# Start of a conformer layer laid out by channel and computed in pairs, and a new place on ACT for three weight splits

## Chip, cores and metric

One core of a Trainium2 chip. The metric is the device time of one execution in microseconds (us), the median of the runs of the kernel. It was 1515.53 us (3 runs, 1515.49 to 1515.91) before the change.

## The reference

Two layers on x of 256 tokens by 1024 channels, all in float32, each sub-layer steered by a vector c (adaLN): a convolution module, a dense feed-forward part, then attention and a mixture of experts. The change lies in the first sub-layer and at the start of the second:

```python
c_act = jax.nn.silu(c)
sh1, sc1, g1, sh2, sc2, g2 = jnp.split(c_act @ ada_w[l] + ada_b[l], 6, axis=-1)
h = x * (1.0 + sc1[:, None, :]) + sh1[:, None, :]
a, g = jnp.split(h @ w_in + b_in, 2, axis=-1)
u = a * jax.nn.sigmoid(g)
u = depthwise_conv(u, w_dw, width=31, causal=True) + b_dw
out = jax.nn.silu(layer_norm(u, g_n, b_n)) @ w_out + b_out
x = layer_norm(ALPHA * x + (1.0 + g1[:, None, :]) * out, ln_g[l, 0], ln_b[l, 0])
h = x * (1.0 + sc2[:, None, :]) + sh2[:, None, :]
f = swiglu(h, ffn_w13[0], ffn_w2[0])
```

(`depthwise_conv` stands for the call of `conv_general_dilated`.)

## The kernel before

Every product of float32 values is made of three matmuls (`mm3`, L203 to L207): high half by high half, low half of the weight by high half, high half of the weight by low half. Weights come as tiles of 1 MB (128 x 2048 numbers) from a packed stream, through six raw buffers; SyncE (SP) issues the transfers in order (L173). `split` (L179) makes the high half on ScalarE (ACT, L189), and the low half by a subtraction on VectorE (DVE) or, for the tiles named in `SPLIT_POOL`, on GpSimd (POOL), at L194. Three pairs of buffers hold the halves. The order of work on each engine is set by the framework's scheduler, steered by `after(...)`, which keeps an instruction from being issued ahead of the given ones. TensorE (PE) takes its instructions strictly in the order given to it.

The stretch that the change touches, up to about 172 us, runs so:

- Start (L117 to L157): c, the taps of the depthwise convolution and six small vectors are loaded as rows, and transposed by PE into columns (`dwT`, `cols`). PE multiplies the adaLN weights with c in `Ada.step` (L226), by 1 MB tile: the scale first, four tiles, then the shift. x (`xtm`, L493) is loaded by token and transposed by PE (`to_dmajor`). `modulate` scales it (`hs`, L343 to L347), in high and low halves.
- Input projection: 8 tiles of 256 columns (`ci`), 48 matmuls each (`cip`). The first two (`FIRST`) are multiplied with the scaled x alone; the shift's share of them is computed apart (`shw`, L524, and L531), and added as a bias `cin` (L535). The others wait for the full h. Then the gate: `sg` (L597) and `U` (L600).
- Depthwise convolution of 31 taps, eight blocks of 128 channels shared out between DVE (`cvv`, L553), ACT with POOL (`pr`, L566, and additions into `dw`, L567) and PE (`cv`, L574, with diagonal matrices `dg` that ACT makes, L481).
- Norm of the convolution's output: transposes and statistics (`cn_tr`, L640), square root (`cn_w`, L354), rows of factors (`cn_rows`, L674), the affine step on dw (L683), z = silu (L688) with its high and low halves (L690, L691).
- Output projection `cout_a` with four weight tiles (`cout`); the norm of the result in `post_ln` (L366 to L388, `xh`), transposes (`x_tr`), the affine steps of the next sub-layer (`h_f`, L343, `h_h`, L345) and then the first feed-forward chunk: `ffn_up`, products with the tiles fa (`fap`) and fb.

Of the kernel before, what the change touches and what calls it, by code (L numbers as in the profile page):

```python
# [19 lines left out]
P = 128  # L20
# [24 lines left out]


# [38 lines left out]
def build(ctx: ExitStack, tc: tile.TileContext, a: dict, dbg: dict | None = None):  # L85
# [26 lines left out]
    def sideps(name):  # L112
# [3 lines left out]
    crows = small.tile([KB, P], F32, tag="crows", name="crows", bufs=1)  # L116
    nc.sync.dma_start(crows[:], a["c"][0].rearrange("(k p) -> k p", p=P))  # L117
    dwrows = tmp.tile([124, 2, P], F32, tag="g32", name="dwrows")
    nc.scalar.dma_start(dwrows[:], a["conv_dw_w"][0].rearrange("j (k p) -> (j k) p", p=P)
                        .rearrange("(u r) p -> r u p", u=2))  # L120
# [8 lines left out]
    ps = mmps("ps_c")  # L129
    nc.tensor.transpose(ps[:, :KB], crows[:], ident[:KB, :KB])  # L130
    cact = cpool.tile([P, KB], F32, name="cact")
    nc.scalar.activation(cact[:], ps[:, :KB], AF.Sigmoid)
    nc.vector.tensor_tensor(cact[:], cact[:], ps[:, :KB], op=ALU.mult)
    crep = cpool.tile([P, KB, 32], F32, name="crep")
    nc.vector.tensor_copy(crep[:], cact[:, :, None].to_broadcast([P, KB, 32]))

    rows = tmp.tile([104, P], F32, tag="h32", name="rows")
    off = 0
    for nm, n in (("conv_in_b", 16), ("conv_dw_b", 8), ("conv_norm_g", 8), ("conv_norm_b", 8), ("ln_g", 32),
                  ("ln_b", 32)):  # L140
# [363 lines left out]
    with after(la):  # L504
        conv_diag(CONV_TENSOR[1][0], 0)
# [810 lines left out]
```

## Time and profile before

| | |
|---|---|
| median of 3 runs | 1515.53 us (1515.49 to 1515.91) |
| the profiled execution's own time | 1517.09 us |
| its span | 1515.3 us |
| PE busy | 1468.2 us, 97% of the span |
| DVE busy | 1262.5 us, 83% |
| ACT busy | 980.9 us, 65% |
| POOL busy | 82.8 us, 5% |
| mean granted clock of PE | 0.989 |
| data read and written | 484.51 MB, mean 320 GB/s |

The profile records one execution. A busy share is an average over the span, and the stretches have different limits: windows give the busy time stretch by stretch, the timeline gives single instructions with what ended the idle time before them (in square brackets), and the tile view gives all instructions on one buffer. PEclk is the granted clock of TensorE, 1.00 for 2.4 GHz and 0.50 for 1.2 GHz. Lengths of matmuls overlap, since they are pipelined.

### The profile page before, as it was taken

How to read it: one execution, taken by the hardware profiler on the slowest of the kernel's cores; microseconds unless marked ns; L12 is line 12 of the kernel's file. 1: busy time of each engine (PE TensorE's matmuls, PEld its weight loads, DVE VectorE, ACT ScalarE, POOL GpSimd, SP SyncE). 2: the span in 40 equal slices, each digit the busy share in tenths (PEclk: the TensorE clock that was granted, in tenths of full speed). 3: DMA queues.
4: the chain of work that ended last, by engine and by line, in shares of the span. 5: the costliest groups of instructions: out<-in, count | busy, mean ns of one | idle time of the engine just before them, and what ended most of it. 6: DMA issues, size and time to landing. Idle time of an engine off the chain costs nothing. (4 is left out here: it accounts for less than half of the span.)

```text
span 1515.3 us, 20370 instructions
## 1 busy us (share of the span) xinstructions
PE 1468.2 (97%) x8018; PEld 1213.2 (80%) x8018; DVE 1262.5 (83%) x1271; ACT 980.9 (65%) x944; POOL 82.8 (5%) x86
## 2 busy tenths in 40 slices
PE   6998999999999999999999999999999999999995
PEld 4886899997967787888888888888888888887884
DVE  2897798757776889899888899988889988888886
ACT  5665444344565776777776677776777777777673
POOL 0692100001001000000000000000000000000000
PEclk9999999999999999999999999999999999999998
DMA  9766699856962788999999999999999999999991
GB/s 356 273 282 226 236 359 336 315 223 269 333 248 85 281 342 331 377 361 354 350 355 348 380 360 353 339 369 356 367 373 359 333 361 363 363 367 345 351 358 52
DMA packets 73380, 484.51 MB, mean 320 GB/s; under 512 B 9044, under 2 KB 11452, under 8 KB 17468
## 3 DMA queue, kind: packets, MB, share of 16 engines
q1 hardware_dynamic: 72848, 482.94, 85.0%
q8 instruction: 65, 1.06, 0.3%
q14 instruction: 39, 0.32, 0.1%
q10 hardware_dynamic: 428, 0.18, 0.0%
HBM read 482.04 MB, written 1.05 MB: 319 GB/s over the span
## 5 line engine op out<-in xcount | busy, mean ns | idle before, releaser
L194 DVE TENSOR_TENSOR eu_l<-eu,eu_h 128x2048 fp32r<-128x2048 f32 (+1 forms) x232 | 507.9, 2213 | 41.4 <-ACT eu_h L189 40.8
L189 ACT ACTIVATE eu_h<-eu 128x2048 fp32r<-128x2048 f32 (+1 forms) x232 | 425.6, 1855 | 89.6 <-PE eup L206 62.5
L207 PE MATMUL eup<-eu_l,g_x 128*128 128x512 f32 x896 | 354.2, 397 | 1.9 <-DVE eu_l L194 1.5
L205 PE MATMUL eup<-eu_h,g_x 128*128 128x512 f32 x896 | 350.6, 391 | 1.8 <-ACT eu_h L189 1.8
L206 PE MATMUL eup<-eu_h,g_x 128*128 128x512 f32 x896 | 349.8, 390 | 0.0
L194 DVE TENSOR_TENSOR e_l<-e,e_h 128x2048 fp32r<-128x2048 f32 (+1 forms) x114 | 251.1, 2212 | 26.0 <-ACT e_h L189 25.7
L189 ACT ACTIVATE e_h<-e 128x2048 fp32r<-128x2048 f32 (+1 forms) x114 | 210.2, 1854 | 21.7 <-PE eup L206 19.6
L207 PEld LDWEIGHTS eup<-eu_l,g_x 128*128 128x128 f32 x896 | 168.2, 188 | 44.1 <-DVE eu_l L194 10.4
L205 PEld LDWEIGHTS eup<-eu_h,g_x 128*128 128x128 f32 x896 | 168.4, 188 | 36.0 <-ACT eu_h L189 2.9
L206 PEld LDWEIGHTS eup<-eu_h,g_x 128*128 128x128 f32 x896 | 168.2, 188 | 35.8
L206 PE MATMUL eo<-e_h,egt 128*128 128x512 f32 x440 | 171.9, 391 | 0.0
L205 PE MATMUL eo<-e_h,egt 128*128 128x512 f32 x440 | 171.5, 391 | 0.0
L207 PE MATMUL eo<-e_l,egt 128*128 128x512 f32 x440 | 156.4, 397 | 0.0
L205 PEld LDWEIGHTS eo<-e_h,egt 128*128 128x128 f32 x440 | 82.6, 188 | 18.3 <-ACT e_h L189 0.4
L206 PEld LDWEIGHTS eo<-e_h,egt 128*128 128x128 f32 x440 | 82.6, 188 | 17.5
L207 PEld LDWEIGHTS eo<-e_l,egt 128*128 128x128 f32 x440 | 79.9, 188 | 15.5 <-issue 0.5
L1059 ACT ACTIVATE egt<-ept 128x512 fp32r<-128x512 f32 x56 | 33.2, 592 | 85.7 <-PE ept L1055 85.7
L1051 ACT ACTIVATE es<-eup 128x512 f32<-128x512 f32 x56 | 33.3, 594 | 42.3 <-PE eup L207 42.0
L1086 POOL TENSOR_TENSOR e_last_l<-e_last,e_last_h 128x1024 fp32r<-128x1024 f32 x1 | 3.0, 2993 | 997.2 <-ACT e_last_h L1084 997.2
L1052 DVE TENSOR_TENSOR eg<-es,eup 128x512 f32<-128x512 f32 x56 | 38.3, 683 | 17.6 <-PE eup L207 17.6
L205 PE MATMUL fap<-h_h,fa_h 128*128 128x256 f32 x176 | 48.9, 280 | 0.9 <-DVE h_h L345 0.9
L206 PE MATMUL fap<-h_h,fa_l 128*128 128x256 f32 x176 | 48.9, 279 | 0.0
(399 smaller groups left out, 2400.5 us busy)
## 6 DMA issues: line engine op xcount, KB each, us to landing
eu<-in_stream_dram SPq DMA_DIRECT2D x216, 1024.0 KB
e<-in_stream_dram SPq DMA_DIRECT2D x106, 1024.0 KB
e_w<-in_stream_dram SPq DMA_DIRECT2D x46, 1024.0 KB
fa<-in_stream_dram SPq DMA_DIRECT2D x11, 1024.0 KB
fb<-in_stream_dram SPq DMA_DIRECT2D x11, 1024.0 KB
f<-in_stream_dram SPq DMA_DIRECT2D x11, 1024.0 KB
ekv_w<-in_stream_dram SPq DMA_DIRECT2D x8, 1024.0 KB
eu<-in_stream_dram SPq DMA_DIRECT2D x16, 512.0 KB
```

Source lines behind the costliest of these rows:

```text
L189: ia = nc.scalar.activation(hi[:, ks], raw[:, ks], AF.Copy)
L194: iv = (sub or nc.vector).tensor_tensor(lo[:, ks, us], raw[:, ks, us], hi[:, ks, us].bitcast(F32), op=ALU.subtract)
L205: nc.tensor.matmul(out, lh, rh, start=start, stop=False)
L206: nc.tensor.matmul(out, ll, rh, start=False, stop=False)
L207: return nc.tensor.matmul(out, lh, rl, start=False, stop=stop)
L1051: nc.scalar.activation(s[:], pa[:], AF.Silu)
L1052: nc.vector.tensor_tensor(g[:], s[:], pb[:], op=ALU.mult)
L1059: ia = nc.scalar.activation(ghf, pt[:], AF.Copy)
L1086: (nc.gpsimd if (n, k0) == (1, 0) else nc.vector).tensor_tensor(lo[:, k0:k1], raw[:, k0:k1], hi[:, k0:k1].bitcast(F32), op=ALU.subtract)
```

## The change

- c, the taps, the small vectors and the scale's bias are laid out by channel ahead of the launch (`by_channel`) and loaded with one transfer (`sm`). x is loaded by channel (`xch`); its copy by token (`xtm`), which the residual needs, is loaded after the gate. The transposes at the start go.
- The scale is computed from four tiles of 256 columns (`scale_sum`: 16 matmuls of 64 x 128 each). After each tile one transpose gives the scale of two blocks of channels (`scale_blocks`), ACT and DVE make their `hs`, and PE multiplies these with the first tile (`first_products`: 12 matmuls).
- Three tiles are multiplied with the scaled x alone (`FIRST`), the third in two halves. The shift's share takes 48 matmuls, not 32.
- POOL splits only one tile, `ci4_0`, in two pieces. Half of the diagonals for the second block on PE are made earlier.
- The splits of the third and fourth output weight tile are issued after the last z (`after(iz)`). The first feed-forward splits are issued after the norm's activation and after the affine steps (`ln_act`, `gate`).

Where a kernel line is quoted below it is the new one. On SP, the start of the program; before:

```order
L117 DMA crows<-in_c_dram 8x128
L173 DMA e_w_143<-in_stream_dram 128x2048
L173 DMA e_w_145<-in_stream_dram 128x2048
L173 DMA e_w_147<-in_stream_dram 128x2048
L493 DMA xtm<-in_x_dram 128x2x1024
L173 DMA e_w_174<-in_stream_dram 128x1024 x2
L260 DMA e_b_209<-in_ada_b_dram 128x1x256
L173 DMA ci_0_260<-in_stream_dram 128x1024 x2
L173 DMA e_w_269<-in_stream_dram 128x2048
```

and with the change (`sc` is a tile of scale weights, `xch` the x by channel, `e_w` a tile of shift or scale weights in the old manner):

```order
L130 DMA sm<-in_small_dram 128x368
L161 DMA sc_97<-in_stream_dram 128x2048
L491 DMA xch<-in_xt_dram 128x2048
L161 DMA ci_0_100<-in_stream_dram 128x2048
L161 DMA sc_102<-in_stream_dram 128x2048
L161 DMA sc_104<-in_stream_dram 128x2048
L161 DMA sc_106<-in_stream_dram 128x2048
L161 DMA ci_0_108<-in_stream_dram 128x2048
L248 DMA e_b_407<-in_ada_b_dram 128x1x256
```

The scale came as four tiles of e_w with x between them; now its first tile, x and the first projection tile come ahead of the other three. On ACT, from the square root of the convolution's norm to z; before:

```order
L354 ACTIVATE cn_w<-cn_mv,eps 128x2
L189 ACTIVATE cout_h<-cout_1329 128x2048
L189 ACTIVATE cout_h<-cout_1327 128x2048
L688 ACT_TABLE_LOAD
L688 ACTIVATE z_1411<-dw,cols 128x256 x2
L690 ACTIVATE z_h<-z_1411 128x512
L688 ACTIVATE z_1418<-dw,cols 128x256 x2
L690 ACTIVATE z_h<-z_1418 128x512
```

and with the change:

```order
L342 ACTIVATE cn_w<-cn_mv,eps 128x2
L765 ACT_TABLE_LOAD
L765 ACTIVATE z_1438<-dw,sm 128x256 x2
L767 ACTIVATE z_h<-z_1438 128x512
L765 ACTIVATE z_1445<-dw,sm 128x256 x2
L767 ACTIVATE z_h<-z_1445 128x512
L765 ACTIVATE z_1452<-dw,sm 128x256 x2
L767 ACTIVATE z_h<-z_1452 128x512
L765 ACTIVATE z_1459<-dw,sm 128x256 x2
L767 ACTIVATE z_h<-z_1459 128x512
L177 ACTIVATE cout_h<-cout_1354 128x2048
L177 ACTIVATE cout_h<-cout_1356 128x2048
```

The two high halves of the output weights and the table load have changed places around z. On ACT, at the norm behind the output projection; before:

```order
L189 ACTIVATE fa_1_h<-fa_1_1710 128x2048
L189 ACTIVATE fb_0_h<-fb_0_1818 128x2048
L354 ACT_TABLE_LOAD
L354 ACTIVATE xh_0_w<-xh_mv_1630,eps 128x1
L354 ACTIVATE xh_1_w<-xh_mv_1648,eps 128x1
L388 ACTIVATE xh_1622<-xh_1622,xh_nm_1638,xh_0_w 128x1024
L343 ACTIVATE h_f_1685<-x_tr_1658,aff_B,aff_A 128x256 x2
L343 ACTIVATE h_f_1690<-x_tr_1659,aff_B,aff_A 128x256 x2
L343 ACTIVATE h_f_1695<-x_tr_1660,aff_B,aff_A 128x256 x2
L343 ACTIVATE h_f_1700<-x_tr_1661,aff_B,aff_A 128x256 x2
L189 ACTIVATE fb_1_h<-fb_1_1824 128x2048
```

and with the change:

```order
L342 ACT_TABLE_LOAD
L342 ACTIVATE xh_0_w<-xh_mv_1657,eps 128x1
L342 ACTIVATE xh_1_w<-xh_mv_1675,eps 128x1
L378 ACTIVATE xh_1649<-xh_1649,xh_nm_1665,xh_0_w 128x1024
L177 ACTIVATE fa_1_h<-fa_1_1737 128x2048
L331 ACTIVATE h_f_1712<-x_tr_1685,aff_B,aff_A 128x256 x2
L331 ACTIVATE h_f_1717<-x_tr_1686,aff_B,aff_A 128x256 x2
L331 ACTIVATE h_f_1722<-x_tr_1687,aff_B,aff_A 128x256 x2
L331 ACTIVATE h_f_1727<-x_tr_1688,aff_B,aff_A 128x256 x2
L177 ACTIVATE fb_0_h<-fb_0_1845 128x2048
L177 ACTIVATE fb_1_h<-fb_1_1851 128x2048
```

fa_1_h moved from ahead of the norm to behind its activation, and fb_0_h from ahead of the norm to behind the affine steps.

```diff
-FIRST = 2
-SPLIT_POOL = ("ci2_0", "ci4_0", )
+FIRST = 3
+SPLIT_POOL = ("ci4_0", )
...
-    conv_diag(CONV_TENSOR[0][0], 0)
-    conv_diag(CONV_TENSOR[0][0], 1)
     e00 = ada_group(0, 0, "e00")
-    e00.step(1, 3)
-    nc.sync.dma_start(xtm[:], a["x"][0].rearrange("(t p) d -> p t d", p=P))
-    e00.step(1)
-    cols = columns()
-    xps = to_dmajor(xtm, "x")
-    c00c = ada_cols(e00.done(1), "c00c")
...
+    load_scale(0)
+    nc.sync.dma_start(xch[:], a["xt"])
+    rawf = [load(win.tile(0, KB, in_cols(0), 256), [KB, 256], "ci0_0")]
+    for g in range(1, 4):
+        load_scale(g)
+    rawf.append(load(win.tile(0, KB, in_cols(1), 256), [KB, 256], "ci1_0"))
+    e00.fetch(0)
...
+    def scale_sum(g):
+        with after(*ipe):
+            for k in range(KB):
+                for m in range(2):
+                    ipe[:] = [nc.tensor.matmul(scps[64 * m:64 * m + 64, g * P:(g + 1) * P], crep64[:, k, :],
+                                               raws[g][:, k, m * P:(m + 1) * P], start=(k == 0), stop=(k == KB - 1))]
...
+    scale_sum(0)
+    la, lv = scale_blocks(0)
+    with after(la, lv):
+        wfirst.append(split(rawf[0], [KB, 256], "ci0_0", parts=2))
+    first_products(0)
+    scale_sum(1)
+    for g in range(1, 4):
+        if g < 3:
+            scale_sum(g + 1)
+        la, lv = scale_blocks(g)
+        first_products(g)
+    with after(la, lv):
+        wfirst.append(split(rawf[1], [KB, 256], "ci1_0", parts=2))
+    with after(*ipe):
+        im = dmajor([psfirst[1]], wfirst[1:2], hs)
+    with after(im):
+        e00.step(0)
...
+    im = half(2, 0)
+    with after(im):
+        c00h = ada_cols(e00e, "c00h")
+    half(2, 1)
...
-        with after(*(behind if t > FIRST else [ishp])):
+        with after(*(behind + iu if t > FIRST else [ishp])):
...
+    xtm = act.tile([P, NT, D], F32, tag="xtm", name="xtm")
+    nc.sync.dma_start(xtm[:], a["x"][0].rearrange("(t p) d -> p t d", p=P))
...
+    conv_diag(CONV_TENSOR[1][0], 0)
     conv_tensor(*CONV_TENSOR[0])
...
     for q in (2, 3):
-        wout.append(split(rout[q], [2, D], f"cout{q}", q == 3, behind=[lz]))
+        with after(iz):
+            wout.append(split(rout[q], [2, D], f"cout{q}", q == 3, behind=[lz]))
...
-        wb = colchunk(w13, FF + c0, width, f"fb{c0}")
+        with after(*gate):
+            wb = colchunk(w13, FF + c0, width, f"fb{c0}")
...
-            with after(last[1]):
-                nxt = ffn_up(c0, 512, lead)
+            with after(last[1], *ln_act):
+                nxt = ffn_up(c0, 512, lead, last)
```

## Rows read from the trace of the kernel before

**Rows 1.** First part of the page: busy time, share of the span, instructions.

```profile
PE 1468.2 (97%) x8018; PEld 1213.2 (80%) x8018; DVE 1262.5 (83%) x1271; ACT 980.9 (65%) x944; POOL 82.8 (5%) x86
```

**Rows 2.** Windows: length, busy us (instructions) of PE, PEld, DVE, ACT, POOL, PEclk, DMA share, GB/s.

```profile
24.00:50.00 26.00, 23.89 (x196) 18.31 (x196) 12.41 (x15) 12.62 (x27) 4.85 (x2) 0.88 0.98 382
50.00:93.00 43.00, 41.47 (x393) 37.34 (x392) 37.49 (x72) 30.20 (x56) 34.51 (x34) 1.00 0.52 200
93.00:124.00 31.00, 31.00 (x148) 27.18 (x149) 29.21 (x75) 20.47 (x48) 26.59 (x28) 1.00 0.62 256
124.00:137.00 13.00, 8.64 (x116) 4.63 (x114) 8.22 (x26) 7.05 (x8) 0.00 (x0) 0.96 0.95 339
172.00:1515.00 1343.00, 1318.16 (x6897) 1094.13 (x6897) 1145.34 (x1031) 880.25 (x746) 10.69 (x7) 0.99 0.87 326
```

**Rows 3.** Timeline of PE, 0 to 32 us: start, length, instruction, idle before.

```profile
7.87 1.94 PE L232 MATMUL e_ps<-e_w,crep 128*32 128x256 f32 x16 [2.03 <-DMA e_w<-in_stream_dram]
...
13.03 1.94 PE L232 MATMUL e_ps<-e_w,crep 128*32 128x256 f32 x16 [0.50 <-DMA e_w<-in_stream_dram]
...
30.58 1.07 PE L232 MATMUL e_ps<-e_w,crep 128*32 128x256 f32 x16
```

**Rows 4.** Tiles cip, cv, cvv, dw: ns min/median/max, first and last start, shape.

```profile
L207 PE MATMUL cip<-hs_l,ci_h x32: 278/283/582, 24.6 to 45.4; 128*128 128x256 f32 x32
...
L206 PE MATMUL cip<-h_h,ci_l x96: 276/276/385, 49.9 to 87.2; 128*128 128x256 f32 x96
...
L574 PE MATMUL cv<-U,dg x140: 377/378/483, 92.8 to 123.0; 128*128 128x256 f32 x140
...
L553 DVE SCALAR_TENSOR_TENSOR cvv<-U,dwT,cvv x111: 471/475/491, 58.7 to 120.6; 128x256 f32<-128x256 f32 x111
...
L567 POOL TENSOR_TENSOR dw<-dw,pr x55: 724/736/2847, 61.1 to 110.6; 128x256 f32<-128x256 f32 x55
```

**Rows 5.** Timeline, 126 to 138 us.

```profile
126.90 0.30 ACT L354 ACTIVATE cn_w<-cn_mv,eps 128x2 f32<-128x2 f32 x1 [5.20 <-DVE cn_mv L659]
...
130.82 3.33 DVE L683 TENSOR_TENSOR dw<-dw,cn_rows 128x512 f32<-128x512 f32 x5 [1.45 <-PE cn_rows L674]
...
132.03 1.91 ACT L189 ACTIVATE cout_h<-cout 128x2048 fp32r<-128x2048 f32 x1 [1.93 <-DMA cout<-in_stream_dram]
...
133.96 1.28 ACT L688 ACT_TABLE_LOAD   x1
...
135.25 1.09 ACT L688 ACTIVATE z<-dw,cols 128x256 f32<-128x256 f32 x2
...
137.12 1.22 PE L205 MATMUL cout_a<-cout_h,z_h 128*128 128x512 f32 x2 [3.84 <-ACT z_h L690]
```

**Rows 6.** Windows of the tile cout_a alone.

```profile
137.00:142.60 5.60, 5.48 (x13) 4.32 (x14) 0.00 (x0) 0.50 1.01 420
...
142.60:163.00 20.40, 19.67 (x85) 15.46 (x83) 2.20 (x4) 1.00 0.46 165
```

**Rows 7.** Timeline, 161 to 172 us.

```profile
161.26 1.92 ACT L189 ACTIVATE fb_h<-fb 128x2048 fp32r<-128x2048 f32 x1 [7.64 <-PE cout_a L206]
...
163.19 1.28 ACT L354 ACT_TABLE_LOAD   x1
...
166.95 1.23 ACT L388 ACTIVATE xh<-xh,xh_nm,xh_w 128x1024 f32<-128x1024 f32 x1
...
169.57 1.93 ACT L343 ACTIVATE h_f<-x_tr,aff_B,aff_A 128x256 f32<-128x256 f32 x4 [1.40 <-PE x_tr L330]
...
171.11 0.38 PE L205 MATMUL fap<-h_h,fa_h 128*128 128x256 f32 x1 [0.92 <-DVE h_h L345]
```

**Rows 8.** Windows of the tile cip alone, columns as in rows 2.

```profile
54.80:93.00 38.20, 30.51 (x262) 29.84 (x261) 3.48 (x8) 3.28 (x8) 1.00 0.50 192
```

**Rows 9.** Timeline of DVE, 40 to 82 us.

```profile
45.36 4.27 DVE L345 CAST h_h<-h_f 128x512 fp32r<-128x512 f32 x1 [2.46 <-ACT h_f L343]
...
79.25 2.69 DVE L194 TENSOR_TENSOR ci_l<-ci,ci_h 128x2048 fp32r<-128x2048 f32 x1 [4.30 <-POOL dw L567]
```

More of the change, by code (lines that the diff above doesn't have):

```diff
@@ new lines, in build, with load_scale @@
+    scps = sideps("sc_ps")
+    raws = []
+    def load_scale(g):
+        raws.append(load(e00.w.tile(0, KB, D + g * 256, 256), [KB, 256], f"sc{g}"))
+    load_scale(0)
[5 more added lines that the diff above has]
+    e00.fetch(0)
+    rawf += [load(win.tile(0, KB, in_cols(t), 256), [KB, 256], f"ci{t}_0") for t in range(2, FIRST)]
@@ new lines, in build, with low @@
+    A = small.tile([P, KB], F32, tag="affA", name="aff0_A", bufs=4)
+    dgs[CONV_TENSOR[0][0], 0] = act.tile([P, 16, P], F32, tag="cd", name="dg_first", bufs=4)
+    hs_h = act.tile([P, KB, S], F32R, tag="big0", name="hs0_h")
+    hs_l = [tmp.tile([P, KB // 2, S], F32R, tag="gm", name=f"hs0_l{u}") for u in range(2)]
+    hs = (hs_h, hs_l)
+    psfirst = [accps(f"cip{t}") for t in range(FIRST)]
+    wfirst, im = [], None
+    def low(k):
+        return hs_l[k // 4][:, k % 4, :]
+    ipe, scale_row = [], {}
@@ new lines, in scale_blocks @@
+    def scale_blocks(g):
+        pst = mmps(f"sct{g}")
+        with after(*ipe):
+            ipe[:] = [nc.tensor.transpose(pst[:, :P], scale_row.pop(g)[:], ident[:])]
+        two = slice(2 * g, 2 * g + 2)
+        nc.vector.scalar_tensor_tensor(A[:, two], pst[:, :P].rearrange("p (m r) -> p m r", m=2)[:, :, 0], 1.0, scb[:, two],
+                                       op0=ALU.add, op1=ALU.add)
+        for k in (2 * g, 2 * g + 1):
+            la = nc.scalar.activation(hs_h[:, k, :], xch[:, k, :], AF.Copy, scale=A[:, k:k + 1])
+            lv = nc.vector.scalar_tensor_tensor(low(k), xch[:, k, :], A[:, k:k + 1], hs_h[:, k, :].bitcast(F32),
+                                                op0=ALU.mult, op1=ALU.subtract)
+        return la, lv
@@ new lines, in first_products @@
+    def first_products(g):
+        wh, wl = wfirst[0]
+        with after(*ipe):
+            for k in (2 * g, 2 * g + 1):
+                for f in range(2):
+                    fs = slice(f * P, (f + 1) * P)
+                    im = mm3(psfirst[0][:, f * S:(f + 1) * S], (wh[:, k, fs], wl[:, k, fs]), (hs_h[:, k, :], low(k)),
+                             k == f == 0, k == KB - 1 and f == 1)
+        ipe[:] = [im]
+    scale_sum(0)
+    la, lv = scale_blocks(0)
+    with after(la, lv):
+        wfirst.append(split(rawf[0], [KB, 256], "ci0_0", parts=2))
@@ new lines, in build @@
+    first_products(0)
[7 more added lines that the diff above has]
+        wfirst.append(split(rawf[1], [KB, 256], "ci1_0", parts=2))
+    with after(*ipe):
+        im = dmajor([psfirst[1]], wfirst[1:2], hs)
+    with after(im):
+        e00.step(0)
+    with after(last_split[0]):
+        conv_diag(CONV_TENSOR[0][0], 0)
+    for t in range(2, FIRST):
+        with after(la, lv):
+            wfirst.append(split(rawf[t], [KB, 256], f"ci{t}_0", parts=2))
@@ new lines, in build, with half @@
+    with after(*last_split):
+        conv_diag(CONV_TENSOR[0][0], 1)
+    e00e = e00.done(0)
+    def half(t, f):
+        wh, wl = wfirst[t]
+        for k in range(KB):
+            im = mm3(psfirst[t][:, f * S:(f + 1) * S], (wh[:, k, f * P:(f + 1) * P], wl[:, k, f * P:(f + 1) * P]),
+                     (hs_h[:, k, :], low(k)), k == f == 0, k == KB - 1 and f == 1)
+        return im
+    im = half(2, 0)
+    with after(im):
+        c00h = ada_cols(e00e, "c00h")
+    half(2, 1)
+    xps = [xch[:, 2 * q:2 * q + 2, :].rearrange("p k s -> p (k s)") for q in range(KB // 2)]
```

108 lines of the change are left out of this document (47 added, 61 removed).

## The prediction

> **What bounds the kernel now.** I read the page's busy shares first: TensorE (PE) works 97% of the span [rows 1]. A kernel like that gets faster only where PE waits or works slowly, so the windows come next [rows 2]. Behind 172 us PE is busy 1318 of 1343 us at a DMA share of 0.87, and but for splits of the first feed-forward chunk nothing in the change touches that stretch; of the roughly 172 us ahead of it, PE has 8.6 busy of 13 us at 124 to 137 and works at a mean granted clock of 0.88 at 24 to 50. Both edits lie there, and whatever they save ahead of the second feed-forward chunk shifts all behind it, because from there on both programs have the same order on PE and the stretch hangs on PE. Then the timelines. In the start, three scale tiles of 1 MB are each met by PE as they land, at 7.87 to 13.03 us (2.6 us a tile), and each takes 1.94 us, where the same instructions take 1.07 at 30.58, once the clock is up [rows 3]. Products of the input projection with the scale alone run from 24.6 to 45.4 us, the first ones also at the low clock [rows 4]. Further on PE sits idle 3.84 us for z's high half [rows 5], works its first 13 matmuls of the output projection in 5.6 us at a clock of 0.50 (the 1.2 GHz level), and the rest at 1.00 [rows 6].
>
> **Part B, the scalar engine behind the convolution.** Now ACT does: high half of output weight (1.91, ends 133.94), table load (1.28), two z (1.09, to 136.34), z's high half, and PE starts 0.78 later, at 137.12 [rows 5]. The split waits for its transfer until 132.03, and the table load stands behind it. z itself needs dw, of which DVE makes five steps from 130.82 in 3.33 us, 0.67 each, two to a pair of channel blocks, so the first pair is ready at 130.82 + 2 x 0.67 = 132.15 [rows 5]. With both splits behind all z, the table load stands behind the square root of 126.90 [rows 5] and is over by about 128.5, hidden. Then z runs 132.15 to 133.24 and PE starts 0.78 later, at about 134.0: **-3.1 us**. PE then waits 0.8 instead of 3.84 us, and before had its low clock right behind that idle time. I take it that the clock stays at 2.4 GHz: 13 matmuls at 0.42 (5.48 / 13) become 13 at 0.23 (19.67 / 85) [rows 6], 13 x 0.19 = **-2.5 us**. If the clock still falls, this is nil.
>
> What is queued behind the moved work: the two splits follow z's last half. z takes ACT four times about 1.75 us from 132.15, to 139.2, so the splits end at 141.1 and 143.0, and their low halves on DVE (2.3 each) about 145.6. PE comes to the third weight tile behind 48 matmuls, 134.0 + 48 x 0.23 = 145.0; its products with high halves need only ACT. So I set a wait at nothing, with a bound of 0.6 us above (145.6 - 145.0).
>
> The norm behind the projection: before, fb_h was split on ACT from 161.26 to 163.18 and the table load started at 163.19, after the statistics [rows 7]. With the gate there is nothing ahead of it, worth up to 1.0. In return fa_1_h (1.92) is put between the norm's pass and the affine steps; the transposes of PE run in it, and of the 1.4 us that ACT waited for them [rows 7] it uses the whole and passes it by 0.5. Net **-0.5 us**, from -1.0 to +0.5. Then fb's two high halves come after the affine steps, 3.8 us of ACT, while PE has 96 matmuls of fa to do: hidden. B: 3.1 + 2.5 + 0.5 = **-6.1 us**. Bounds: 3.1 - 0.6 - 0.5 = 2.0 (clock falls, all waits come) and 3.1 + 2.5 + 1.0 = 6.6.
>
> **Part A, the start.** Taken away: the transposes of c, x, the small rows and the taps, and ACT's small transfers; the added 1 MB of x for the residual is read at 50 to 93 us, where the DMA share is 0.52 [rows 2], so it costs nothing. Added: 16 matmuls of 64 columns out by 128 in for each of four scale tiles. Before, a scale tile is 8 of 32 columns by 256, four side by side in the array, and now two side by side; the same numbers pass in twice the time, so a tile takes up to twice 1.94 and 1.07 [rows 3]: I put 3.6 at the low clock and 1.9 at the high one, since the last end counts once. I lay it out at 2.6 us a transfer: scale 0 lands at 7.9, x 10.5, tile 0 13.1, scales 1 to 3 15.7, 18.3, 20.9, tile 1 23.5. PE: scale 0 at the low clock to 11.5; transpose, scale, hs on ACT and DVE; first 12 products 14.4 to 17.5; scale 1 to 20.6; from there I put the clock up (PE has then worked nearly without a break), so scale 2 to 22.5, products of pair 2 to 25, scale 3 to 27, pairs 3 and 4 to 32. Tile 1's split runs to 33.2, its 48 matmuls at 0.115 to 38.7 (before 45.4 [rows 4]). Four shift tiles (1.07 each, [rows 3]) end at about 43, tile 2 in halves with the shift's columns between at 48.4, the shift's 48 products at 53.9, tile 3's low half at 55.2.
>
> So at 55.2 five tiles of 48 remain. Before, at 54.8, 261 of the projection's matmuls remained [rows 8], 21 more than 240. Those 21 are 2.4 us (0.115 each, half of the 0.23 for 512 columns); less 0.4, 2.0 us are won. From 54.8 to the last one's end near 87.5 [rows 4] are 32.7 us, and 261 x 0.115 are 30.0: 2.7 went to other work and waits, and of these I count 2.1 as gone, since the shift's small sums and the low halves are made earlier against their need. The convolution on PE, which starts at 92.8 [rows 4], starts **4.1 us** earlier. Its other parts must keep up. DVE is busy 29.2 of 31 us there [rows 2]; its U waits for the shift 1.8 us longer, but the 4.30 us in which its low half of a tile stood for a POOL addition [rows 9] go, since the last tile's low half is due before POOL's additions bind it. Its taps, last begun at 120.6 [rows 4], then begin their last 1.8 to 2.5 us earlier, near 118.5, and end near 119. POOL's additions, last begun at 110.6 [rows 4], now stand behind some 17 diagonals and one high half of ACT (6.5 us by the order, at 0.29 and 1.9 each) and end near 118, just under the transposes at 119.2. I take **-3.7 us**; bounds: +0.5 (DVE and POOL hold the end where it was and the later U shows) and -5 (tile 3 isn't waited for either).
>
> One row speaks against part A. DVE's cast of 128x512 took 4.27 us, 45.36 to 49.63, while POOL did its low half, and a low half of DVE beside POOL additions 2.69 [rows 9]. The change has POOL's low half of tile 4 at about 54 to 59, beside DVE's low half of tile 3. The Trainium skill ("SBUF — State Buffer", section "SBUF: two separate sides") says that the port pair that the two share is locked for a whole instruction, and that whoever comes second waits it out; the 4.27 us cast agrees with that. I have DVE first, since tile 3's high half precedes tile 4's on ACT, so the sum has nothing for it. If POOL is first, one of its two pieces (about 2.3 us, half of the 4.27) goes ahead of tile 3: -3.7 becomes -1.4.
>
> **Sum.** 6.1 + 3.7 = 9.8 us off a profiled span of 1515.3, which gives 1505.5. The profiled execution took 1517.09, 1.6 above the median of 1515.53; the difference lies around the span, so I take the 9.8 off the median: **1505.7 us**.
>
> **Rivals.**
> 1. *The front gives nothing*: PE reaches the convolution earlier, but DVE (29.2 of 31 busy) or POOL ends as before. For it: those shares. Against: the 4.30 us wait that goes. 1515.5 - 6.1 = 1509.4.
> 2. *The clock falls again at the output projection*, or the third weight tile is late: B is 3.1 + 0.5 = 3.6. 1515.5 - 3.6 - 3.7 = 1508.2. For it: the idle stretch isn't quite gone. Against: it is 0.8 and not 3.84.
> 3. *POOL takes the port first* (above): 1505.7 + 2.3 = 1508.0.
> 4. *The other side: the clock stays low in the front.* PE works in short pieces between transfers and pairs there, and before it was at 0.88 in the mean over 24 to 50 with far longer runs [rows 2]. Each us at the low level from 21 on does half a us of work. From the 9.8 forecast, low to 21 + 19.6 = 41 us is the point at which all gain is eaten; low to 50 costs 14.5: 1520.2. Against: behind 30.58 PE's clock was up, with pieces of products between shift tiles [rows 3].
> 5. *The change doesn't do what it says*: the fine pairs wait on ACT and DVE in turn so that tile 0 ends as late as tile 1 does now. That is rival 1 in its time.
>
> **Chances.** Forecast (1503.5 to 1507) 0.50; rivals 1 and 5 0.17; 2 0.10; 3 0.07; parts lost in both A and B, within 3 us of now, 0.09; rival 4 0.07. The best case is 1515.5 - 6.6 - 5 = 1503.9, and mixes of 1 and 2 come to 1515.5 - 3.6 + 0.5 = 1512.4. The range **1502.5 to 1511.5** goes a little past the best case, whose terms are no exact bounds, and leaves out rival 4 and the worst of the mixes. Within 0.2% (3.0 us, about what a measurement of this kernel can tell from no change): 0.09. Faster 0.84, slower 0.07.
>
> **What would show it.** PE's output projection starts about 7 us earlier and its wait for z's high half is under 1 us (before 3.84); its windows show clock 1.00 throughout; the table load lies before z's dw; the cv tile starts near 88.7, cn_tr near 119.5; the first fap starts near 161.3 (171.11 less 9.8); the stretch behind is the same length. Wrong would be: cv starting early and cn_tr not (rival 1); PEclk 0.50 at the output projection (2); a DVE low half above 4 us near 55 (3); PEclk 0.50 between 25 and 45 (4); or a stretch behind 172 us that has grown, which would mean that transfers set the time there.

## The result, and the profile after

The changed kernel took 1508.48 us, the median of 6 runs (1506.44 to 1511.43), beside 1515.96 us for the kernel before on the same chips (1515.49 to 1520.02). The ratio is 0.9946, with a 95% interval from 0.9931 to 0.9960. A second series, further down, gave 0.9938 (0.9924 to 0.9953). The forecast was 1505.7 us, faster; the range went from 1502.5 to 1511.5. The profiled execution has a span of 1509.4 us, 5.9 less than before.

The windows of the changed kernel, columns as in the rows of before:

```profile
24.00:50.00 26.00, 23.85 (x239) 20.49 (x238) 10.14 (x19) 17.95 (x46) 0.30 (x1) 1.00 0.86 339
50.00:93.00 43.00, 43.00 (x400) 37.90 (x399) 38.63 (x78) 33.39 (x70) 32.03 (x34) 1.00 0.74 286
93.00:124.00 31.00, 30.93 (x165) 26.66 (x167) 28.42 (x75) 20.60 (x48) 26.91 (x29) 1.00 0.51 203
124.00:137.00 13.00, 11.59 (x116) 7.25 (x109) 9.92 (x27) 8.31 (x15) 0.00 (x0) 1.00 0.97 364
172.00:1509.00 1337.00, 1313.50 (x6833) 1089.10 (x6831) 1137.86 (x1023) 876.60 (x741) 10.68 (x7) 0.99 0.87 326
```

Compare these with [rows 2]. PEclk is 1.00 from 24 us on, where it was 0.88 at 24 to 50. At 124 to 137 us PE is busy 11.59 us, not 8.64. The last window has the same DMA share of 0.87; it begins at the same time and ends with the span, so its length shows only that the span is shorter. Counted from the first product of fa, 1344.2 us follow before and 1346.2 now.

The timeline at z, which answers to [rows 5]:

```profile
124.72 0.30 ACT L342 ACTIVATE cn_w<-cn_mv,eps 128x2 f32<-128x2 f32 x1 [5.20 <-DVE cn_mv L736]
...
125.03 1.28 ACT L765 ACT_TABLE_LOAD   x1
...
128.63 3.33 DVE L760 TENSOR_TENSOR dw<-dw,cn_rows 128x512 f32<-128x512 f32 x5 [1.45 <-PE cn_rows L751]
...
130.08 1.09 ACT L765 ACTIVATE z<-dw,sm 128x256 f32<-128x256 f32 x2 [3.77 <-DVE dw L760]
...
131.95 0.97 PE L193 MATMUL cout_a<-cout_h,z_h 128*128 128x512 f32 x3 [0.85 <-ACT z_h L767]
```

The table load now starts at 125.03, right behind the square root. z starts as soon as DVE has made the first pair of dw, and PE starts at 131.95 after 0.85 us of waiting, not 3.84. The first 5.6 us of the output projection, which were at 0.50 [rows 6], read:

```profile
131.90:137.50 5.60, 5.55 (x24) 4.43 (x25) 0.00 (x0) 1.00 0.99 360
```

In the 5.6 us in which PE did 13 matmuls, it now does 24, at 1.00. Behind this, PE never waits for a half of an output weight: the tile view of cout_a has waits for z's halves and for PE alone. The timeline behind the projection, answering to [rows 7]:

```profile
158.74 1.23 ACT L378 ACTIVATE xh<-xh,xh_nm,xh_w 128x1024 f32<-128x1024 f32 x1
...
159.87 1.90 ACT L177 ACTIVATE fa_h<-fa 128x2048 fp32r<-128x2048 f32 x1
...
161.67 1.91 ACT L331 ACTIVATE h_f<-x_tr,aff_B,aff_A 128x256 f32<-128x256 f32 x4
...
163.18 0.39 PE L193 MATMUL fap<-h_h,fa_h 128*128 128x256 f32 x1 [1.20 <-DVE h_h L333]
```

The start, where [rows 3] were scale tiles of another form, as PE sees it:

```profile
6.25 3.29 PE L516 MATMUL sc_ps<-sc,crep 128*64 128x128 f32 x32 [6.25 <-DMA sc<-in_stream_dram]
...
12.45 0.58 PE L193 MATMUL cip<-hs_h,ci_h 128*128 128x256 f32 x1 [2.14 <-ACT ci_h L177]
...
16.35 3.35 PE L516 MATMUL sc_ps<-sc,crep 128*64 128x128 f32 x32
...
20.10 1.97 PE L516 MATMUL sc_ps<-sc,crep 128*64 128x128 f32 x32 [0.40 <-DVE sce L519]
...
28.05 0.39 PE L193 MATMUL cip<-hs_h,ci_h 128*128 128x256 f32 x1 [0.79 <-ACT hs_h L530]
```

Tile 0's products begin at 12.45 us (24.0 before), each later pair of blocks waits 0.79 us for ACT, and the clock rises between the second scale tile (3.35 us) and the third (1.97 us): its mean is 0.60 in the window from 16 to 20 us and 1.00 from 20 to 24. Last, the convolution on PE and the transposes behind it (tile view), for [rows 4]:

```profile
L646 PE MATMUL cv<-U,dg_first x32: 377/378/483, 90.7 to 97.5; 128*128 128x256 f32 x32
...
L716 PE MATMUL cn_tr<-ident,dw x16: 271/272/299, 121.0 to 122.9; 128*128 128x128 f32 x16
```

It starts at 90.7 us, where it was 92.8, and the transposes at 121.0, where they were 123.2.

To compare whole programs, I cut the span at seven starts that the tile views give: the first cn_tr, the first and last product of the output projection (cout_a), the first of fa, the first of ff_a (behind the second chunk's products), the last of wo_a and the first of eup (expert products). The table has the length of each stage in us, good to 0.1, from one profiled execution of each kernel; the kernels are described with the experiments.

| kernel | to cn_tr | to cout_a | cout_a | to fa | to ff_a | to end of wo_a | to eup | the rest |
|---|---|---|---|---|---|---|---|---|
| before | 123.2 | 13.9 | 25.3 | 8.7 | 44.7 | 274.5 | 16.7 | 1008.3 |
| changed | 121.0 | 10.9 | 23.0 | 8.3 | 46.1 | 275.0 | 18.3 | 1006.8 |
| z only | 124.3 | 10.9 | 23.0 | 8.7 | 46.2 | 274.5 | 16.6 | 1008.4 |
| norm only | 123.3 | 13.8 | 24.3 | 9.2 | 44.7 | 274.7 | 18.2 | 1008.2 |
| both on ACT | 124.1 | 10.9 | 23.0 | 8.3 | 44.7 | 276.1 | 18.3 | 1008.3 |
| front only | 121.7 | 13.1 | 24.4 | 8.7 | 46.1 | 275.0 | 13.9 | 1008.2 |
| filled wait | 124.4 | 13.9 | 23.7 | 8.6 | 44.7 | 274.7 | 15.1 | 1007.4 |
| fa broken | 120.9 | 11.0 | 23.0 | 8.2 | 45.3 | 274.7 | 15.1 | 1006.8 |
| laid out | 123.1 | 13.3 | 24.3 | 8.7 | 44.7 | 274.9 | 18.2 | 1006.4 |
| two tiles | 122.4 | 10.9 | 23.2 | 8.3 | 44.7 | 275.0 | 18.3 | 1006.5 |
| changed again | 121.9 | 10.9 | 23.0 | 8.2 | 44.8 | 274.8 | 16.6 | 1006.8 |
| logits apart | 120.6 | 11.0 | 22.9 | 8.3 | 46.2 | 275.3 | 18.5 | 1006.7 |
| fa behind | 121.1 | 11.0 | 22.9 | 8.0 | 46.9 | 275.1 | 13.9 | 1007.1 |

From before to changed, the stages up to fa give 2.2 + 3.0 + 2.3 + 0.4 = 7.9 us. Then 1.4 are lost ahead of ff_a, 0.5 up to wo_a and 1.6 at the routing, and 1.5 come at the end: 7.9 - 3.5 + 1.5 = 5.9, the difference of the spans. The first stage scatters from one execution to the next: cn_tr comes at 123.2 to 124.4 in the five kernels with the front as it was (laid out and two tiles are in between, and not counted), and at 120.6 to 121.9 in the six with the new one.

### The profile page after: what moved, and what is told of

Read it like the earlier page. It is cut to its first block, busy times and chain, and to the rows that moved or that the text cites. A ratio compares the mean times of both kernels' runs of the same rounds, so it can differ in the third digit from the quotient of the medians.

```text
span 1509.4 us, 20496 instructions
## 1 busy us (share of the span) xinstructions
PE 1469.0 (97%) x8084; PEld 1219.6 (81%) x8084; DVE 1261.0 (84%) x1280; ACT 980.9 (65%) x946; POOL 76.1 (5%) x86
## 5 line engine op out<-in xcount | busy, mean ns | idle before, releaser
L193 PEld LDWEIGHTS eo<-e_h,egt 128*128 128x128 f32 x440 | 82.6, 188 | 18.3 <-ACT e_h L177 0.5
L1130 ACT ACTIVATE es<-eup 128x512 f32<-128x512 f32 x56 | 33.3, 594 | 42.4 <-PE eup L195 42.2
L195 PE MATMUL fbp<-h_l,fb_h 128*128 128x256 f32 x176 | 49.2, 280 | 0.0
```

The costliest lines, as they stand in the source:

```text
L193: nc.tensor.matmul(out, lh, rh, start=start, stop=False)
L195: return nc.tensor.matmul(out, lh, rl, start=False, stop=stop)
L1130: nc.scalar.activation(s[:], pa[:], AF.Silu)
```

## The experiments

The question was which of the four terms are the change's, whether the clock term is what the prediction took it for, and what takes 3.5 us back behind fa. Where a run's ratio is given, it is against the kernel before on the same chip, with its 95% interval.

**z only.** The kernel before, with:

```diff
     for q in (2, 3):
-        wout.append(split(rout[q], [2, D], f"cout{q}", q == 3, behind=[lz]))
+        with after(iz):
+            wout.append(split(rout[q], [2, D], f"cout{q}", q == 3, behind=[lz]))
```

> Kernel before, with only the two output weight splits behind the last z. Theory (front and ACT order add up, and the clock keeps up because PE's wait shrinks): the wait for z's high half falls from 3.84 us to about 0.8, the output projection starts 3.0 us earlier (134.1), the granted clock stays 1.00 in it, worth 2.3 more, and the first product of fa comes near 165.8 (171.1 before); about 1510.3 us. Rival (the clock stays up only because the new front loads PE differently): the start comes 3.0 us earlier, the clock still falls to 0.50, fa near 168.1, about 1512.5 us.

Measured: ratio 0.9970 (0.9954 to 0.9987). The stage from cn_tr to cout_a fell from 13.9 to 10.9 us, and cout_a itself from 25.3 to 23.0. The first 5.6 us of cout_a in this kernel:

```profile
135.20:140.80 5.60, 5.56 (x24) 4.42 (x25) 0.00 (x0) 1.00 1.01 364
```

24 matmuls at 1.00: the old front is no hindrance, and the theory holds. fa came at 166.9, not 165.8, since this execution reached cn_tr 1.1 us later (124.3).

**Norm only.** The kernel before, with only the gates at the norm:

```diff
-                nc.scalar.activation(xhat[:, t, h:], xhat[:, t, h:], AF.Identity, scale=r, bias=nmr[:])
+                ln_act[:] = [nc.scalar.activation(xhat[:, t, h:], xhat[:, t, h:], AF.Identity, scale=r, bias=nmr[:])]
...
-        wb = colchunk(w13, FF + c0, width, f"fb{c0}")
+        with after(*gate):
+            wb = colchunk(w13, FF + c0, width, f"fb{c0}")
...
-            with after(last[1]):
-                nxt = ffn_up(c0, 512, lead)
+            with after(last[1], *ln_act):
+                nxt = ffn_up(c0, 512, lead, last)
```

> Kernel before, with only the first feed-forward splits gated behind the norm's activation and the affine steps. Theory: output projection as before (137.1 us, clock 0.50 at its start), the norm's table load no longer behind fb_h, fa 0.4 us earlier (170.7), about 1515.1 us. Rival (the gate is what saves, since the splits also hold DVE and the raw buffers): fa 2 us or more earlier, 1513.5 or less.

Measured: ratio 1.0010 (0.9998 to 1.0022). The stage behind cout_a took 9.2 us, 0.5 more than before. PE's wait in front of the second half of the transposes (1.8 us) ends with DVE's half of the norm, but this one had to wait for the second square root on ACT, and that stood behind fa_1_h:

```profile
163.56 1.24 ACT L390 ACTIVATE xh<-xh,xh_nm,xh_w 128x1024 f32<-128x1024 f32 x1 [2.62 <-DVE xh_nm L389]
...
164.71 1.90 ACT L189 ACTIVATE fa_h<-fa 128x2048 fp32r<-128x2048 f32 x1
...
166.51 0.28 ACT L354 ACTIVATE xh_w<-xh_mv,eps 128x1 f32<-128x1 f32 x1
...
167.67 0.81 DVE L392 TENSOR_SCALAR xh<-xh,xh_mv,xh_w 128x1024 f32<-128x1024 f32 x1
```

Neither theory nor rival: alone, the gates save nothing here. But the order on ACT is not that of the changed kernel, where both square roots precede fa_1_h (at 154.62 and 158.53, fa_1_h at 159.87), so this run does not tell what the gates are worth in that order.

**Both on ACT.** The two edits above together, with the old front.

> Kernel before, with both moves on ACT and the old front. Theory: sum of the two, fa near 165.4 (5.7 us earlier), about 1509.8 us. Rival (they share one gain): fa as in the run with z's splits alone, 165.8 or later. Rival on the pitch: 256-column products after it at 0.118 instead of 0.113 us, which takes 1.5 to 2 us back by 215 us.

Measured: ratio 0.9950 (0.9934 to 0.9966). The stages are 10.9, 23.0 and 8.3, those of the changed kernel to 0.1 us, and fa came 42.2 us behind cn_tr, where it came 47.9 before: 5.7 us, the number expected. Against z only, the two gates bring 0.4 us here (8.3 for 8.7). The rival on the pitch, the spacing of 256-column products, did not come either: the stage to ff_a took 44.7 us, so ACT's new order can go with the faster spacing. Z only, with half of that order, had 46.2.

**Front only.** The changed kernel with these two edits undone.

> Changed kernel, with ACT's order at z and at the norm as before. Theory: transposes of the convolution's norm start at 121.0 as in the changed kernel (123.2 before), PE waits 3.8 us for z's high half again and the clock falls to 0.50, fa near 168.9, about 1513.3 us. Rival (the front has no part in the gain, which stands in the order on ACT): 1515.5 us.

Measured: ratio 0.9967 (0.9952 to 0.9983). cn_tr came at 121.7. PE's wait was shorter than in the kernel before, but it was there, and cout_a took 24.4 us:

```profile
PE cout_a L193 <- ACT z_h L767: 3.0, 1, 3.0
```

In its first 5.6 us the granted clock was 0.70 in the mean, with 17 matmuls:

```profile
134.80:140.40 5.60, 5.60 (x17) 4.37 (x18) 0.00 (x0) 0.70 1.01 413
```

So the front's part is its own, and the low clock comes back with the wait. The median shows 5.0 us (0.33% of 1517.6), more than the 3.2 that this profile shows at fa (167.9 for 171.1, of which 1.5 lie ahead of cn_tr), and with the 7.6 of both on ACT more than the whole change has. The stage to eup tells why such sums can't be made from medians: it took 13.9 us here, and 16.7 and 18.3 in the first two rows.

**Filled wait.** The kernel before, with work for PE in the time in which it waits for z (the products are thrown away):

```diff
         e02_0 = e02.done(0)
+        fill = mmps("fill")
+        for u in range(3):
+            nc.tensor.matmul(fill[:], ones[:], dgm[:].rearrange("p t c -> p (t c)"), start=True, stop=True)
```

> Kernel before, with three float32 products of 512 columns put on PE ahead of the output projection; they are thrown away and fill about 2.6 of the 3.84 us in which PE waits for z's high half. Theory (the low clock in the output projection comes from PE's idle time): the projection still starts near 137 us after cv's start of 92.8, the granted clock stays 1.00 in it, and it ends 2.3 us earlier against its start (23 us from first start to last start in place of 25.3). Rival (the clock falls for what PE did before 133 us, or only an earlier start of z helps): clock 0.50 at 137 to 142 as before, 25.3 us.

Measured: one run of 1514.29 us. The timeline of PE:

```profile
133.76 2.84 PE L681 MATMUL fill<-cn_dg,ones 128*128 128x512 f32 x6
...
138.33 0.97 PE L205 MATMUL cout_a<-cout_h,z_h 128*128 128x512 f32 x3 [1.10 <-ACT z_h L693]
```

PE works up to 137.2 and waits 1.10 us. cout_a starts 13.9 us behind cn_tr, as before, but it takes 23.7 us, not 25.3, and its first 5.6 us read:

```profile
138.30:143.90 5.60, 5.01 (x20) 3.67 (x21) 0.00 (x0) 1.00 1.01 421
```

The clock is 1.00 although z comes as late as before. Of the 23.7 us, 0.6 are a second pair of products for the gate (G_ps), which the scheduler put into the projection in this kernel. It is one execution, but the other twelve profiles agree: in the four in which PE waited 3.0 to 3.8 us for z (before, norm only, front only, laid out), the granted clock in the first 5.6 us of cout_a was 0.50 once and 0.70 three times; in the eight in which it waited 0.85 us it stayed at 1.00. So it was the idle time that brought the low clock, and the term of the clock is one of its own.

**Fa broken.** The changed kernel, with a break between the products of fa and fb in the first chunk (thrown away):

```diff
-        dmajor(pss, wa, hT)
+        im = dmajor(pss, wa, hT)
+        if c0 == 0:
+            with after(im):
+                for g in range(4):
+                    nc.tensor.matmul(ekv.ps[32 * g:32 * g + 32, 0:P], crep[:, g, :], ident[:], start=True, stop=True)
```

> Changed kernel, with four small products of 128 columns on PE between the first feed-forward chunk's fa and fb; they are thrown away. Theory on the 2 us lost behind 163 us (PE's stream of 256-column products runs at one of two spacings, 0.113 or 0.118 us, and keeps the one it has until something else comes between): fa at 0.118, then fb and the second chunk at 0.113, first product of ff_a 45.2 us after the first of fa (46.1 in the changed kernel, 44.7 before), 1 us less in all, about 1507.5. Rival (the slower spacing comes from what ACT, DVE or the transfers do beside it): 0.118 up to 209 us, nothing gained.

Measured: ratio 0.9942 (0.9923 to 0.9960). The stage to ff_a took 45.3 us, as the theory had it, but not for its reason: the spacing was 0.113 already in the second half of fa, ahead of the break, where the changed kernel has the same instructions at 0.118, and it was 0.113 behind the break too. So the run shows that the same stretch can have the other spacing, and that a break need not change it; the last section has breaks that did.

**Laid out.** The kernel before, with the small vectors, taps, c and x laid out by channel (`by_channel`, `sm`, `xch`, the late `xtm`) and everything else as it was:

```diff
...
-    nc.sync.dma_start(xtm[:], a["x"][0].rearrange("(t p) d -> p t d", p=P))
+    xch = act.tile([P, KB, S], F32, tag="xtm", name="xch")
+    nc.sync.dma_start(xch[:], a["xt"])
     e00.step(1)
-    cols = columns()
-    xps = to_dmajor(xtm, "x")
+    xps = [xch[:, 2 * q:2 * q + 2, :].rearrange("p k s -> p (k s)") for q in range(KB // 2)]
...
```

> Kernel before, with c, x, taps and small vectors laid out by channel and x by token loaded late, the rest (scale by four tiles of e_w, two tiles, ACT's order) as before. Theory (the gain of the front is that products start before the whole scale is there): the last scale tile still lands near 19 us and the first products start at most 2 us earlier than 24.0, the transposes of the convolution's norm start near 122.5 (123.2 before, 121.0 changed), 0 to 1 us gained. Rival (the gain is the transposes and small transfers that are gone): cn_tr near 121, 2 us or more.

Measured: ratio 0.9971 (0.9959 to 0.9983). First products at 23.0 us (24.0 before), cn_tr at 123.1, 0.1 us earlier than before and 0.8 earlier than the mean of the five kernels with the old front (123.9): the transposes that are gone are not where most of the front's gain comes from. The median shows 4 us all the same. Of these the profile has 1.7 up to fa (0.6 of it a shorter wait for z, 1.0 a shorter time at the low clock in cout_a) and nothing at the first eup; the rest is not explained by this profile.

**Two tiles.** The changed kernel with `FIRST = 2`, the third tile's halves and the shift's third part left out:

```diff
-FIRST = 3
+FIRST = 2
...
-    im = half(2, 0)
     with after(im):
         c00h = ada_cols(e00e, "c00h")
-    half(2, 1)
...
```

> Changed kernel with two tiles multiplied with the scaled x alone in place of three (the shift's share in 32 products, not 48). Theory (the third tile covers the time in which the shift is summed and h is made, at the price of 16 products of the shift): PE waits for h behind the shift tiles, some 3 us at 43 to 50, and cv starts near 92 (90.7 changed). Rival (the third tile buys nothing, since DVE's h and the low half of the next tile come at the same time anyway): cv starts at 90.7 or earlier.

Measured: one run of 1511.04 us. cv started at 92.1, near the 92 of the theory. Counted from the first product of tile 0, so that the scatter ahead of it drops out, cv came after 79.6 us, and after 77.1 to 78.4 in the six profiles with three tiles: the third tile saves 1.2 to 2.5 us. PE never waited for h. It waited 0.6 and 0.7 us for the shift's sum (at 43.6 and 44.7), and most of all for a tile of the adaLN weights of the gate, e01, which follow the shift's:

```profile
58.25 1.07 PE L220 MATMUL e_ps<-e_w,crep 128*32 128x256 f32 x16 [2.76 <-DMA e_w<-in_stream_dram]
```

The changed kernel has none of these three waits. So the third tile covers the shift's sum, as the theory had it, and, more than that, a transfer.

**Changed again.** The changed kernel, unaltered.

> The changed kernel once more. Theory (what it loses behind 163 us is chance of an execution: the spacing of 256-column products, 0.113 or 0.118 us, and how long the clock is at 0.50 in the routing stretch near 490 us): up to the first product of fa the profile repeats within 0.5 us (163.2), from there to the first of ff_a either 44.7 or 46.1 us, from ff_a to eup between 289 and 294 us. Rival (both belong to the changed kernel): 46.1 and 293.3 again.

Measured: ratio 0.9938 (0.9924 to 0.9953), median 1507.68 us. cn_tr came at 121.9, 0.9 us later than in the first profile and outside the 0.5 of the theory; the next three stages repeat to 0.1 us, the stage to ff_a took 44.8 us and not 46.1, the routing 16.6 and not 18.3. From fa to the end it is 1343.0 us, 1.2 less than before. The rival falls: what was lost behind fa does not belong to the change.

**Logits apart.** The changed kernel, with two shift tiles of the expert layer moved:

```diff
+            if t != u:
+                with after(*last_mm):
+                    e12.step(1, 1)
...
-    with after(*last_mm):
-        e12.step(1, 2)
```

> Changed kernel with two shift tiles of the expert layer put between the routing's logits instead of behind them, no work added. Theory (the clock falls in the routing because the logits keep PE at products of 8 columns for 3.6 us): clock above 0.90 at 484 to 505 us, but the logits are ready up to 2 us later, so the stretch from the last product of wo_a to the first of eup takes 15 to 16 us (17.9 in the changed kernel's profile, 13.6 where the clock didn't fall, 14.8 in another), time 1506 to 1509. Rival (the clock falls for another cause, such as the chain of waits ahead of it): 0.50 again for 4 to 10 us and 2 us lost, 1510 or more.

Measured: ratio 0.9962 (0.9948 to 0.9976), median 1510.90 us. PE's timeline, without the rows between:

```profile
492.32 1.06 PE L999 MATMUL logits<-rw,yT 128*128 128x8 f32 x8
...
495.32 0.36 PE L1034 MATMUL pos<-M,tri 128*128 128x8 f32 x2 [1.94 <-DVE M L1032]
```

The logits are ready 1.4 us later than in the changed kernel (493.4 for 492.0), PE then waits 1.94 us for the routing, and the granted clock falls behind that wait and is 0.50 from 496 to 502. The stage took 18.5 us. The low clock came all the same, as the rival had it, and nothing was gained: 1510.90 us beside 1507.68 for the changed kernel in the same series. What starts it stays open; in the first profile of the changed kernel it had set in at 490.3, while the logits ran.

**Fa behind.** The changed kernel, with the second fa tile's split behind the affine steps too:

```diff
-            with after(last[1], *ln_act):
+            with after(*last):
                 nxt = ffn_up(c0, 512, lead, last)
```

> Changed kernel with the second fa tile's high half behind the four affine steps, not ahead of them. Theory (behind the norm only 0.4 of 1.5 us came, since fa_1_h, 1.90 us from 159.87, stands ahead of the first affine step, whose transposes are ready 1.1 us earlier): from the last product of the output projection to the first of fa 7.2 us (8.3 in the changed kernel), of which PE loses up to 0.7 again at the 49th product, where fa_1's low half is late; net 0.4 to 1.1 us, too little for the median to tell. Rival (the affine step is held by the transposes on PE, not by ACT): 8.3 us as before, and a later fa_1 that makes the first chunk 1 us longer.

Measured: ratio 0.9945 (0.9931 to 0.9960), median 1508.44 us. The first affine step came at 161.49, behind a wait of 1.40 for the transposes; in the changed kernel it came at 161.67, with fa_1_h ahead of it:

```profile
161.49 1.93 ACT L331 ACTIVATE h_f<-x_tr,aff_B,aff_A 128x256 f32<-128x256 f32 x4 [1.40 <-PE x_tr L318]
...
165.79 1.91 ACT L177 ACTIVATE fa_h<-fa 128x2048 fp32r<-128x2048 f32 x1
...
PE fbp L193 <- ACT fb_h L177: 0.3, 1, 0.3
```

From the last product of the output projection to the first of fa it took 8.0 us, where the changed kernel took 8.3. So the split costs 0.3 us, not 1.1, and the rival is nearer: the transposes hold the affine step. fb's high half is then 0.3 us late for PE, and the first two chunks are some 0.7 us longer (46.9 for 46.1 in the table). None of the versions beats the changed kernel by more than the measurement can tell.

## Why the prediction was right

It named the sign, the two places and the mechanism; one of its four terms, the start, came out 1.0 to 1.5 us too large. Up to the first product of fa, 7.9 of the 9.8 us came. By its own steps:

- **Wait for z (-3.1): -3.0.** The table load, z and PE's start are each where the step put them, and the z-only kernel shows the same with the old front.
- **Clock of the output projection (-2.5): -2.3** in the two profiles shown. It is the step with the least ground in the trace of before ("I take it that the clock stays"), and the filled wait confirms its cause: with PE kept busy and z as late as ever, the clock stays up. Its size is not fixed, though. The kernels that keep the wait took 25.3, 24.3, 24.4 and 24.3 us for cout_a, so 1.3 to 2.3 are saved.
- **Norm (-0.5): -0.4, with both of its parts smaller.** The step took 1.0 for the table load and gave 0.5 back for fa_1_h. Fa behind shows that fa_1_h costs 0.3; with the 0.4 of the whole, that leaves 0.7 for the table load, if the two simply add; no run has the one without the other. That the two were off by about as much is luck.
- **Start (-3.7): mis-sized, -2.2 in the two profiles.** Over the five profiles with the old front (before, z only, norm only, both on ACT, filled wait) cn_tr comes at 123.9 in the mean, over the six with the new one at 121.2, so 2.6 is the better number. From cv to cn_tr all thirteen take 30.3 us, so the difference lies ahead of cv, where 4.1 was forecast and 2.2 came. The layout up to the shift held: PE was done with its products at 54.5, where 53.9 was put. The step that failed is "of these I count 2.1 as gone". The 2.7 us of "other work and waits" that it found in the trace of before were these:

```profile
54.81 1.05 PE L531 MATMUL shw<-ones,shr 2*128 2x1 f32 x8
...
82.00 0.38 PE L206 MATMUL cip<-h_h,ci_l 128*128 128x256 f32 x1 [0.91 <-DVE ci_l L194]
```

  The small sum of the shift (`shw` from `shr`) is 1.0 us of work, six more adaLN products at 69.4 are 0.6, and only the 0.91 for a low half is a wait. It is the one that went: the 4.30 us in which DVE stood for POOL [rows 9] are no longer in the trace, and PE waits nowhere between 54.7 and 90.7. The work stayed, and some was added:

```profile
54.67 1.05 PE L602 MATMUL shw<-ones,shr 2*128 2x1 f32 x8
...
58.38 0.60 PE L602 MATMUL shw<-ones,shr 2*128 2x1 f32 x4
```

  From the small sum to cv PE took 38.0 us before (54.81 to 92.84) and takes 36.0 now (54.67 to 90.66). 22 products fewer are -2.5 and the wait -0.9; the third tile's own small sum is +0.5, a slower spacing of the products +0.7 (in the mean 0.119 us each for 0.116, short breaks included; last section), and the adaLN products, 96 in both, are +0.1. The forecast had no term for the second sum and the spacing. The 36.0 are the same in all six profiles with the new front, and the old one took 36.9 to 38.0 there, so the scatter of the new front lies ahead of 54.7. What the parts of the front bring, single profiles can't split finely: against the mean of the old front, the layout alone has cn_tr 0.8 us earlier, the scale in pairs with it 1.5, and the third tile makes it 2.6.
- **The convolution's other engines: not in the way, so rivals 1 and 5 fall.** DVE's taps (`cvv`) begin their last at 117.4, where 118.5 was put (120.6 before), and PE sets the end. POOL's additions begin their last at 111.1, not near 118: the diagonals ahead of them on ACT cost far less than the order let expect (17 at 0.29 and a split of 1.9 are 6.8 us by the prediction's own numbers, for which it had 6.5).
- **Rival 2, a low clock at the output projection or a late third weight tile: no.** PEclk is 1.00 there, and cout_a has no wait for a weight.
- **Rival 3, POOL first at the port: no.** DVE's half took 2.27 us. POOL started 1.3 us behind it and took 5.55 for its two pieces:

```profile
53.45 2.27 DVE L182 TENSOR_TENSOR ci_l<-ci,ci_h 128x2048 fp32r<-128x2048 f32 x1
...
54.78 5.55 POOL L182 TENSOR_TENSOR ci_l<-ci,ci_h 128x1024 fp32r<-128x1024 f32 x2 [5.35 <-ACT ci_h L177]
```

  In the kernel before, POOL took 4.61 us for a tile of the same size (at 44.51). With the 0.94 from its start to the end of DVE's half that makes 5.55, so the time fits a hold ahead of the first piece. By the Trainium skill ("SBUF — State Buffer", section "SBUF: two separate sides"), of a DVE instruction with two inputs in SBUF and a GpSimd instruction that reads SBUF, the one that starts second waits until the first is done. This row agrees.
- **Rival 4, a low clock in the front: no.** PEclk is 1.00 at 24 to 50. It is with the scale summed as before that the clock can fall once more: in the window from 37 to 47 us its mean is 0.66 to 0.83 in four of these six profiles (norm only, both on ACT, filled wait, laid out) and 1.00 in before and z only; in the seven with the scale in pairs it is 1.00.
- **The median.** 7.0 us below the 1515.5 from which the forecast was made, 7.5 and 8.3 below the kernel before in the same two series (8.2 and 9.4 by the ratios), for 9.8 forecast. The start's 1.0 to 1.5 us is the part that was mis-sized. What remains lies behind fa, where the prediction said the same length: the two profiles of the changed kernel are 2.0 us longer and 1.2 shorter there than before. So how near the median came to the forecast is in part chance.

## What to carry to other kernels

Where TensorE waits ahead of a dense stretch, look at what the engine that it waits for does there that only comes due later: two splits and a table load on ACT cost 3.0 us here, and two lines of issue order took them away. The wait was paid twice, once as idle time and once as a low clock behind it (1.3 to 2.3 us), and float32 products put into it on PE, though thrown away, got the second part back. A stretch that looks like waiting should be read instruction by instruction before it is counted as gone: of 2.7 us here, 0.9 were a wait. And where medians scatter by as much as the parts of an effect, cut the profiles at fixed instructions and compare the stages: in the kernels with both moves on ACT and `fa_1_h` in its place, the three from cn_tr to fa repeat to 0.3 us, while their spans go from 1505.0 to 1513.7.

## What the runs showed of the hardware that was not expected

**The routing's clock.** The stage from wo_a to eup has the same instructions in all kernels but logits apart. It took 13.9 us in the two profiles in which the clock stayed up, and 15.1 to 18.3 in the ten others, in which it fell for part of it. One window over it, of the changed kernel:

```profile
484.60:502.60 18.00, 17.70 (x142) 13.37 (x141) 13.63 (x57) 8.71 (x12) 1.44 (x2) 0.72 0.74 279
```

and of front only:

```profile
489.30:503.00 13.70, 13.04 (x142) 10.57 (x141) 13.30 (x57) 8.71 (x12) 1.38 (x2) 1.00 0.74 288
```

The same 142 PE instructions took 17.70 us at a mean clock of 0.72 and 13.04 at 1.00. Fa behind, with the changed kernel's routing, had 13.9 too. This stage alone can make 4.4 us of difference between two executions. The 28 runs of the kernel before beside the first four experiments are 8.4 us apart, from 1513.46 us at a mean clock of 0.992 to 1521.81 at 0.984. What decides it in an execution stays open.

**Two spacings at the full clock.** In the first two feed-forward chunks, streams of 256-column products run at 0.113 or at 0.118 us each, both at a granted clock of 1.00. The first chunk's fb, before:

```profile
182.76 0.28 PE L206 MATMUL fbp<-h_h,fb_l 128*128 128x256 f32 x1
...
193.42 0.28 PE L207 MATMUL fbp<-h_l,fb_h 128*128 128x256 f32 x1
```

and changed:

```profile
175.03 0.28 PE L194 MATMUL fbp<-h_h,fb_l 128*128 128x256 f32 x1
...
186.09 0.28 PE L195 MATMUL fbp<-h_l,fb_h 128*128 128x256 f32 x1
```

The same 94 steps take 10.65 us in the first and 11.07 in the second, 0.1133 and 0.1178 each. Within fa, both kernels change from one to the other, in opposite directions, at a short break behind the 50th product. In the changed kernel:

```profile
168.91 0.28 PE L195 MATMUL fap<-h_l,fa_h 128*128 128x256 f32 x1
169.02 0.39 PE L193 MATMUL fap<-h_h,fa_h 128*128 128x256 f32 x2
169.25 0.28 PE L193 MATMUL fbp<-h_h,fb_h 128*128 128x256 f32 x1
169.50 0.39 PE L194 MATMUL fap<-h_h,fa_l 128*128 128x256 f32 x1
```

Ahead of this break its products are 0.113 apart and behind it 0.118, up to ff_a at 209.4; before, they are 0.118 apart up to the break and 0.113 behind it. From fa to ff_a, none of the thirteen profiles changes its spacing without such a break. The 334 products behind it, at 0.0044 us each, are 1.5 us, of which the first half of fa gives 0.2 back; the stage to ff_a is 1.4 longer. It is not the kernel's: changed again goes from 0.118 to 0.113 at the same break. The tile view has the median length of these matmuls over all chunks, in the changed kernel

```profile
L194 PE MATMUL fap<-h_h,fa_l x176: 276/281/388, 163.4 to 325.5; 128*128 128x256 f32 x176
```

and in the same kernel's other profile

```profile
L194 PE MATMUL fap<-h_h,fa_l x176: 276/276/337, 164.3 to 324.9; 128*128 128x256 f32 x176
```

What brings one or the other is not known. In the input projection, between 55 and 91 us, all six profiles with the new front have the slower one for most of the stretch, so chance of an execution need not be all of it.
